# Expert hidden layers in two PSUM banks, combination weights and overflow branch placed earlier, tail rewritten

## The chip, the cores and the metric

The kernel runs on one core of a Trainium2 chip. The metric is the device time of one execution in microseconds (us), median of three runs. The profiled execution is one further run, and every duration below comes from it.

## The reference

The reference is one hybrid decoder layer in float32 for 256 tokens of 1024 columns: a conditioned RMS norm, one combined projection that feeds retention and latent attention, a gated merge, and then a hierarchical mixture of experts, whose result goes through a last RMS norm. The change touches only the experts and the last norm:

```python
h = h + gate2 * hier_moe(u)      # u: (256 tokens, 1024)
# hier_moe: top-1 of 4 groups, top-2 of its 8 experts; for each expert e of 32
#   hid = silu(u @ w1[e]) * (u @ w3[e])      # 1024 -> 256
#   y   = hid @ w2[e]                        # 256 -> 1024
#   out[token] += weight(token, e) * y[token]
out = h * rsqrt(mean(h * h) + 1e-6) * final_norm
```

All 32 experts have to be read: each has three float32 matrices of 1 MB.

## The kernel before

The experts are worked on in eight batches (`bt` 0 to 7) of four experts with 32 token slots each. The four experts of a batch lie side by side on the 128 partitions, as column tiles of 32 slots. For one batch the kernel does this:

- `hidden` calls `hidden_mm` (L1391, matmul L1403) for w1 and then for w3. Both write one PSUM bank, w1 into columns 0 to 255 and w3 into 256 to 511. Then come tanh on ACT (L1495), two products on DVE (L1496, L1497), two transposes on PE (L1501) and a copy on ACT (L1504).
- `combine_weights` (L1450) multiplies the selection matrices with the weights (DVE L1456), transposes them (PE L1457) and copies the result to `GT` (ACT L1458).
- `gather` builds the slots of the next batch (DVE L1337 and L1339, PE L1343 and L1354).
- `expert_out` (L1508) multiplies with w2 (PE L1514), applies the gate (DVE L1517) and adds through `GT` into the four banks `fin` (PE L1523), which hold the layer's result: `fin[2*b+h]` is half h of token block b.

After batch 7's `hidden` stands an overflow branch (L1546 to L1602): each engine reads a count (`values_load`, L1548) and branches (L1549). It is taken only if an expert has over 32 tokens, which is not so in the run profiled.

The tail (from L1605) is w2 of batch 7 in five column pieces q0 to q4, cut at 0, 256, 512, 768, 896 and 1024. `last_mm(q)` multiplies (PE L1622) and applies the gate (DVE L1625). `last_sum(q)` adds through `GT` into `fin` (PE L1632) and squares on ACT (L1635), with a second ACT instruction that reads the accumulated sum; the squares of q3 and q4 are taken together. `last_gain(q)` multiplies a piece in `fin` by the norm's gain into the output tile (DVE L1639). Then the sums go through a reduction and a scale (DVE L1655, L1656), one small DVE step per token block (L1659), a power of -1/2 on POOL per block (L1660), and the scaling of the output: ACT L1664 and DVE L1666 for the first half of the columns, DVE L1668 straight from `fin` for the second. Four transfers of 256 KB go out from SP (L1667, L1669).

What sets the order: weights are loaded by SP in the order of a plan made in a first pass, into 27 SBUF slots; a load is issued when its slot has been released and the load eight issues earlier has landed. Loads of w1, w2 and w3 are issued at L249, the last pieces of w2 at L311. Matmuls of a constant (L387, `keep_warm`) stand between the last batch's quarters of w3. Within the experts, PE and DVE follow a planner that puts an instruction as early as its inputs and engine allow; in the tail DVE, ACT and POOL follow the order in which the code is written. Waits between engines are set by tile: two engines that touch the same PSUM bank wait for each other, whatever the columns.

Of the kernel before, what the change touches and what calls it, by code (L numbers as in the profile page):

```python
# [18 lines left out]
D = 1024  # L19
# [185 lines left out]
def body(ctx, tc, A, out, plan=None):  # L205
# [1183 lines left out]
    ph_of = [None]  # L1389

    def hidden_mm(bt, m, ks):  # L1391

        name = ("w1", "w3")[m]
        ph = ph_of[0]
        cut = (name, bt) in QB
        for k in ks:
            c = k // 2 if cut else 0
            for j in range(4):
# [4 lines left out]
                i = T.matmul(ph.t[32 * j:32 * j + 32, m * 256:(m + 1) * 256], ug[:, k, 32 * j:32 * j + 32], w,  # L1403
# [29 lines left out]
    ph_of[0] = bank()  # L1433
# [29 lines left out]
    def hidden(bt):  # L1463
        if bt:
            ph_of[0] = bank()
        ph = ph_of[0]
# [58 lines left out]

    for bt in range(8):
        hdT = hidden(bt)
# [6 lines left out]
        if bt:  # L1534
            combine_weights(bt)
# [10 lines left out]
    f_s = {n: SL.alloc("f_" + n) for n in ("x2", "u2", "ov", "w1", "w3", "w2", "hid")}  # L1546
    Gov, Gsh = (f_s["hid"].t[:, i:i + 64].rearrange("p (b e) -> p b e", b=2) for i in (1536, 1600))
    many = nc.values_load(cnti[0:1, 0:1], min_val=0, max_val=256)  # L1548
    with tc.If(many > CAP):  # L1549
        V.scalar_tensor_tensor(Gov, rk1, float(CAP), Gt, op0=ALU.is_gt, op1=ALU.mult)  # L1550
        x2 = f_s["x2"].t.rearrange("p (b k q) -> p b k q", b=2, k=8)
        u2 = f_s["u2"].t.rearrange("p (k t) -> p k t", k=8)
        ov = f_s["ov"].t.rearrange("p (b n) -> p b n", b=2)
        V.memset(f_s["ov"].t, 0.0)
        for b in range(2):
            V.tensor_scalar(x2[:, b], hp[:, b], rstd2[:, b:b + 1], None, op0=ALU.mult)
        for k2 in range(4):
            pb = bank()
            for kk in range(2):
                for b in range(2):  # L1560
                    T.transpose(pb.t[:, kk * 256 + b * 128:kk * 256 + (b + 1) * 128], x2[:, b, 2 * k2 + kk, :], ident)
            for kk in range(2):
                k = 2 * k2 + kk
                S.activation(u2[:, k, :], pb.t[:, kk * 256:(kk + 1) * 256], AF.Identity, bias=s2c[:, k:k + 1],
                             scale=a2c[:, k:k + 1])
            pb.free()
        wv = {n: f_s[n].t.rearrange("p (k n) -> p k n", k=8 if n != "w2" else 2) for n in ("w1", "w3", "w2")}
        ft, fh = f_s["hid"].t[:, 0:512], f_s["hid"].t[:, 512:1024].rearrange("p (f t) -> p f t", f=2)
        fy = f_s["hid"].t[:, 1024:1536]
        with tc.For_i(0, 32, 1) as e:  # L1570
            for n in ("w1", "w3", "w2"):
                src = A[n][0].rearrange("g i (p k) n -> (g i) p k n", p=128)
                Q.dma_start(wv[n], src[bass.ds(e, 1)].rearrange("o p k n -> (o p) k n"))
            ph = [bank(), bank()]
            for m, n in enumerate(("w1", "w3")):
                for f in range(2):
                    for k in range(8):
# [5 lines left out]
            for pb in ph:  # L1583
                pb.free()
# [16 lines left out]
    for s in f_s.values():  # L1601
        s.free()  # L1602
# [109 lines left out]
```

## Time and profile before

| | us |
|---|---|
| median of 3 runs | 521.34 (520.93 to 521.62) |
| profiled execution, its own time | 521.56 |
| its span | 519.8 |
| PE busy | 492.7 (95%) |
| DVE busy | 286.4 (55%) |
| ACT busy | 197.9 (38%) |

The profiled execution lies 0.22 us above the median, and 1.8 us of its time lie outside the span. The span is read from its end: the stretch from about 350 us is the expert loop, the stretch from 503 us the tail. For each stretch the table of stretches gives the DMA share (of 16 engines), the GB/s and the clock that TensorE was granted; the waits say what an engine stood still for; the timeline gives the tail instruction by instruction.

### The profile page before, as it was taken

To read this page: it belongs to the slowest core of one execution; us is meant where nothing else is said; L and a number is where in the kernel's file an instruction comes from. 1 tells how busy PE (TensorE), PEld (TensorE's weight loads), DVE (VectorE), ACT (ScalarE), POOL (GpSimd) and SP (SyncE) were. 2 spreads that over 40 slices of the span, in tenths; PEclk is the share of its full clock that TensorE was granted. 3 is DMA by queue.
4 is the path that set the end of the run, shared out by engine and by line. 5 is a ranking of instruction groups with operands and counts; after the bars stand their busy time and mean duration, and the time that the engine had idled before them with its cause. 6 is when DMAs were issued, how large, how long until landed. Compare 5 with 4: busy or idle time off the path is not lost.

```text
span 519.8 us, 8582 instructions
## 1 busy us (share of the span) xinstructions
PE 492.7 (95%) x3440; PEld 339.1 (65%) x3443; DVE 286.4 (55%) x525; ACT 197.9 (38%) x366; POOL 56.8 (11%) x50
## 2 busy tenths in 40 slices
PE   6899999999999999999999999999999989898994
PEld 2678999997887878888688887443344343434432
DVE  3455789884696987979966746414031313131213
ACT  3545773454677544557434424202020211121013
POOL 1000321411000001119800000000000000000000
PEclk9999999999999999999999999999999999999999
DMA  9999899788876782998689888999999999999992
GB/s 272 323 320 361 297 353 398 289 321 312 333 242 244 247 321 81 338 396 308 234 342 352 311 352 301 417 386 422 420 417 419 421 415 419 421 419 416 392 325 99
DMA packets 68097, 174.85 MB, mean 336 GB/s; under 512 B 5422, under 2 KB 27091, under 8 KB 57816
## 3 DMA queue, kind: packets, MB, share of 16 engines
q1 hardware_dynamic: 65602, 174.01, 89.8%
q10 hardware_dynamic: 2454, 0.27, 0.4%
q8 instruction: 28, 0.46, 0.4%
q14 instruction: 13, 0.11, 0.1%
HBM read 173.22 MB, written 1.05 MB: 335 GB/s over the span
## 4 chain that ended last, share of the span: by engine, by line
PE 74%; DVE 8%; DMA 6%; SPq 5%; ACT 3%; issue 2%; POOL 1%; ACTq 1%; DVEq 0%; POOLq 0%
PE b L1403 11%; PE b L378 8%; PE b L380 8%; PE b L379 8%; PE b L1514 6%; PE b L1523 5%; PE b L1343 5%; SPq L249 3%; DVE s L464 3%; DMA s<-in_w_in 2%; SPq L241 2%; DMA s<-in_w 2%; PE b L1354 1%; PE b L1543 1%; ACT s L463 1%
## 5 line engine op out<-in xcount | busy, mean ns | idle before, releaser
L464 DVE TENSOR_TENSOR s<-s,s 128x1024 fp32r<-128x1024 f32 (+2 forms) x92 | 110.9, 1219 | 41.5 <-ACT s L463 40.5
L463 ACT ACTIVATE s<-s 128x1024 fp32r<-128x1024 f32 (+2 forms) x92 | 83.3, 922 | 86.9 <-PE b L380 53.7
L378 PE MATMUL b<-s,s 128*128 128x512 f32 (+2 forms) x258 | 102.2, 396 | 1.3 <-ACT s L463 1.3
L380 PE MATMUL b<-s,s 128*128 128x512 f32 (+2 forms) x258 | 99.4, 385 | 1.3 <-DVE s L464 1.3
L379 PE MATMUL b<-s,s 128*128 128x512 f32 (+2 forms) x258 | 98.1, 380 | 0.0
L1403 PE MATMUL b<-s,s 128*32 128x256 f32 x1024 | 61.4, 380 | 0.0
L378 PEld LDWEIGHTS b<-s,s 128*128 128x128 f32 x258 | 48.5, 188 | 15.6 <-ACT s L463 4.4
L380 PEld LDWEIGHTS b<-s,s 128*128 128x128 f32 x258 | 48.4, 188 | 13.2 <-DVE s L464 3.8
L379 PEld LDWEIGHTS b<-s,s 128*128 128x128 f32 x258 | 48.5, 188 | 8.5 <-issue 0.2
L1403 PEld LDWEIGHTS b<-s,s 128*32 128x32 f32 x1024 | 32.8, 110 | 31.1 <-issue 9.9
L1061 DVE SCALAR_TENSOR_TENSOR s<-s,cs,s 128x1024 f32<-128x1024 f32 x32 | 41.4, 1293 | 0.3
L532 PE MATMUL b<-s,s 128*128 128x256 f32 x128 | 36.2, 284 | 0.5 <-DVE s L464 0.5
L530 PE MATMUL b<-s,s 128*128 128x256 f32 x128 | 36.4, 285 | 0.0
L531 PE MATMUL b<-s,s 128*128 128x256 f32 x128 | 36.1, 283 | 0.0
L1495 ACT ACTIVATE wr<-b 128x256 f32<-128x256 f32 x8 | 3.1, 383 | 78.5 <-PE b L1403 73.7
L1514 PE MATMUL b<-s,wr 128*32 128x512 f32 x224 | 32.8, 596 | 0.0
L1343 PE MATMUL b<-s,sml 128*128 128x512 f32 x56 | 26.9, 603 | 5.3 <-DVE sml L1339 5.3
L1337 DVE TENSOR_TENSOR S<-cst,rk 128x128 f32<-128x128 f32 x16 | 4.1, 287 | 48.9 <-PE b L1457 48.9
L1130 POOL TENSOR_TENSOR s<-s,s 128x1024 f32<-128x1024 f32 x8 | 25.8, 3260 | 13.0 <-DVE s L464 13.0
L1523 PE MATMUL b<-s,rt 128*128 128x512 f32 x56 | 26.2, 611 | 0.0
L372 ACT ACTIVATE s<-b 128x512 f32<-128x512 f32 (+2 forms) x25 | 14.1, 568 | 31.0 <-PE b L1343 12.5
L532 PEld LDWEIGHTS b<-s,s 128*128 128x128 f32 x128 | 24.4, 191 | 0.9 <-DVE s L464 0.9
(258 smaller groups left out, 654.7 us busy)
## 6 DMA issues: line engine op xcount, KB each, us to landing
s<-in_w SPq DMA_DIRECT2D x92, 1024.0 KB
s<-in_w_in SPq DMA_DIRECT2D x22, 1024.0 KB
s<-in_w_ada SPq DMA_DIRECT2D x16, 1024.0 KB
s<-in_w_ada SPq DMA_DIRECT2D x16, 512.0 KB
s<-in_w_mla_o SPq DMA_DIRECT2D x4, 1024.0 KB
s<-in_w_ret_o SPq DMA_DIRECT2D x4, 1024.0 KB
s<-in_w_out SPq DMA_DIRECT2D x4, 1024.0 KB
s<-in_w SPq DMA_DIRECT2D x6, 512.0 KB
```

The lines of the kernel that those rows point to most:

```text
L378: T.matmul(o, l[0], r[0], start=start, stop=False, skip_group_check=True)
L379: T.matmul(o, l[1], r[0], start=False, stop=False, skip_group_check=True)
L380: return T.matmul(o, l[0], r[1], start=False, stop=stop, skip_group_check=True)
L463: S.activation(hi, src, AF.Copy)
L464: V.tensor_tensor(lo, src, hi, ALU.subtract)
L530: T.matmul(o, hi[:, f], mh, start=k == 0 and c == 0, stop=False, skip_group_check=True)
L532: T.matmul(o, lo[:, f], mh, start=False, stop=k == 7, skip_group_check=True)
L1061: V.scalar_tensor_tensor(a, t[:, kk, :], cs[:, k:k + 1], a, op0=ALU.mult, op1=ALU.add)
L1343: T.matmul(pg[k4].t, Sr[:, b], hp[:, b, 4 * k4:4 * k4 + 4, :].rearrange("p k q -> p (k q)"), start=b == 0, stop=b == 1, skip_group_check=True)
L1403: i = T.matmul(ph.t[32 * j:32 * j + 32, m * 256:(m + 1) * 256], ug[:, k, 32 * j:32 * j + 32], w, start=k == 0, stop=k == 7, skip_group_che ...
L1514: T.matmul(py[n].t[32 * j:32 * j + 32, :], hdT[:, k, 32 * j:32 * j + 32], ts[j][:, k, n * 512:(n + 1) * 512], start=k == 0, stop=k == 1, s ...
L1523: T.matmul(fin[2 * b + n].t, GT[:, b * 128:(b + 1) * 128], y[:, n * 512:(n + 1) * 512], start=bt == 0, stop=bt == 7, skip_group_check=True)
```

## The change

It has four parts. First, `hidden` takes two banks, one for w1 and one for w3; tanh and the first product are written between the two sets of matmuls. Second, `combine_weights(bt)` for batches 1 to 7 is called before `hidden(bt)` instead of behind it. Third, the overflow branch becomes a function, with its body as it was, that is called before `hidden(7)`. Fourth, the tail: PE joins the engines whose order is written by hand; `last_sum(2)` comes before `last_mm(3)`; q3 and q4 are squared separately, q4 of block 1 on DVE (a copy and a product with accumulation); `last_gain` is applied to q2 and q3 too, ahead of `last_sum(4)`; one step and one power serve both blocks; ACT scales 512 columns of each block, DVE 384 and then 128 out of `fin`; one of the four output transfers is issued from ACT's queue.

```diff
-    ph_of = [None]
+    ph_of = [None, None]
...
-        ph = ph_of[0]
+        ph = ph_of[m]
...
-                i = T.matmul(ph.t[32 * j:32 * j + 32, m * 256:(m + 1) * 256], ug[:, k, 32 * j:32 * j + 32], w,
+                i = T.matmul(ph.t[32 * j:32 * j + 32, 0:256], ug[:, k, 32 * j:32 * j + 32], w,
...
         if bt:
-            ph_of[0] = bank()
-        ph = ph_of[0]
+            ph_of[:] = bank(), bank()
+        p1, p3 = ph_of
...
+            if m == 0:
+
+                S.activation(ht, p1.t[:, 0:256], AF.Tanh, scale=0.5)
+                V.scalar_tensor_tensor(ht, ht, 1.0, p1.t[:, 0:256], op0=ALU.add, op1=ALU.mult)
+                p1.free()
...
-        S.activation(ht, ph.t[:, 0:256], AF.Tanh, scale=0.5)
-        V.scalar_tensor_tensor(ht, ht, 1.0, ph.t[:, 0:256], op0=ALU.add, op1=ALU.mult)
-        V.tensor_mul(ht, ht, ph.t[:, 256:512])
-        ph.free()
+        V.tensor_mul(ht, ht, p3.t[:, 0:256])
+        p3.free()
...
     for bt in range(8):
+        if bt:
+            combine_weights(bt)
+        if bt == 7:
+            overflow()
         hdT = hidden(bt)
...
-        if bt:
-            combine_weights(bt)
...
     def last_sum(q):
         for b in range(2):
             T.matmul(fp[b][q], GT[:, b * 128:(b + 1) * 128], y[:, piece[q]], start=False, stop=True, skip_group_check=True)
-            if q != 3:
-                f = fp[b][q] if q < 3 else fin[2 * b + 1].t[:, 256:512]
-                S.activation(sq, f, AF.Square, accum_out=ssf[:, b, min(q, 3):min(q, 3) + 1])
+            f, w = fp[b][q], cut[q + 1] - cut[q]
+            if (q, b) == (4, 1):
+                V.tensor_copy(sq2, f)
+                V.scalar_tensor_tensor(sq2, sq2, 1.0, sq2, op0=ALU.mult, op1=ALU.mult, accum_out=ssf[:, b, q:q + 1])
+            else:
+                S.activation(sq[:, 0:w], f, AF.Square, accum_out=ssf[:, b, q:q + 1])
...
-    tail.enter_context(tc.manual_schedule(engines={V.engine, S.engine, G.engine}))
+    tail.enter_context(tc.manual_schedule(engines={T.engine, V.engine, S.engine, G.engine}))
...
+    last_sum(2)
     last_mm(3)
-    last_sum(2)
     last_mm(4, (0,))
     last_sum(3)
     last_mm(4, (1,))
-    V.tensor_reduce(s3, ssf[:, :, 0:3], AX.X, ALU.add)
+    last_gain(2)
+    V.tensor_reduce(s3, ssf[:, :, 0:4], AX.X, ALU.add)
     V.tensor_scalar(s3, s3, 1.0 / D, EPS, op0=ALU.mult, op1=ALU.add)
+    last_gain(3)
     last_sum(4)
-    for b in range(2):
-        V.scalar_tensor_tensor(tf[:, b:b + 1], ssf[:, b, 3:4], 1.0 / D, s3[:, b:b + 1], op0=ALU.mult, op1=ALU.add)
-        G.tensor_tensor(rf[:, b:b + 1], tf[:, b:b + 1], mhalf[:, 0:1], ALU.pow)
+    V.scalar_tensor_tensor(tf, ssf[:, :, 4], 1.0 / D, s3, op0=ALU.mult, op1=ALU.add)
+    G.tensor_tensor(rf, tf, mhalf[:, 0:2], ALU.pow)
     for b in range(2):
         r = rf[:, b:b + 1]
-        m = 512 if b else 256
-        S.activation(o[:, b, 0:m], o[:, b, 0:m], AF.Copy, scale=r)
-        if b == 0:
-            V.tensor_scalar(o[:, b, m:512], o[:, b, m:512], r, None, op0=ALU.mult)
-        Q.dma_start(out[0, b * 128:(b + 1) * 128, 0:512], o[:, b, 0:512])
-        V.scalar_tensor_tensor(o[:, b, 512:1024], fin[2 * b + 1].t, r, fnb[:, 512:1024], op0=ALU.mult, op1=ALU.mult)
+        S.activation(o[:, b, 0:512], o[:, b, 0:512], AF.Copy, scale=r)
+        V.tensor_scalar(o[:, b, 512:896], o[:, b, 512:896], r, None, op0=ALU.mult)
+        V.scalar_tensor_tensor(o[:, b, 896:1024], fp[b][4], r, fnb[:, 896:1024], op0=ALU.mult, op1=ALU.mult)
+        (S if b else Q).dma_start(out[0, b * 128:(b + 1) * 128, 0:512], o[:, b, 0:512])
         Q.dma_start(out[0, b * 128:(b + 1) * 128, 512:1024], o[:, b, 512:1024])
```

Behind the change the lines are: tanh L1483, first product L1484, second product L1500, transposes L1504, branch L1533 and L1534, `last_mm` L1628 and L1631, `last_sum` L1638 (copy L1641, product with accumulation L1642, squares L1644), `last_gain` L1648, reduction and scale L1665 and L1666, step L1669, power L1670, scaling L1673 to L1675, output L1676 and L1677.

The first place is PE between batch 7's hidden layer and its last layer. In the rows, `wr` is the hidden tile, `rt` is `GT`, `S` the selection matrices and `cnti` the count. Before:

```order
L1501 MATMUL b_4159<-cst,wr 128x128 [waits DVE_49,PE_49]
L1501 MATMUL b_4159<-cst,wr 128x128
...
L1457 MATMUL b_4168<-cst,S_2752 128x128 [waits PE_49]
L1457 MATMUL b_4168<-cst,S_2752 128x128
L1548 TENSOR_LOAD cnti [waits DVE_49]
L1549 COMPARE_AND_BRANCH
...
L1622 MATMUL b_4308<-s_3915,wr 32x256 [waits DVE_49,DMAHW6_49,PE_49,Activation_49]
L1622 MATMUL b_4308<-s_3915,wr 32x256 x3
```

Now:

```order
L1533 TENSOR_LOAD cnti [waits DVE_49]
L1534 COMPARE_AND_BRANCH
...
L1504 MATMUL b_4305<-cst,wr 128x128 [waits DVE_49]
L1504 MATMUL b_4305<-cst,wr 128x128
...
L1628 MATMUL b_4316<-s_3921,wr 32x256 [waits DMAHW6_49,Activation_49]
L1628 MATMUL b_4316<-s_3921,wr 32x256 x3
L1628 MATMUL b_4316<-s_3921,wr 32x256 [waits DMAHW7_49]
```

The count and the branch now stand ahead of batch 7's hidden layer, and the transposes L1457 have left this place as well, so that the first piece's matmuls follow the hidden tile's copy and the constant's matmuls.

The second place is DVE in the tail, from q4's multiplication to the first scaling (before, one row earlier). The `b` tiles of L1648 are the banks of `fin`, `sml` are the small sums. Before:

```order
L1625 TENSOR_TENSOR s_3078<-b_4350,s_664 128x128 [waits PE_49]
L1625 TENSOR_TENSOR s_3078<-b_4364,s_664 128x128 [waits PE_49]
L1655 TENSOR_REDUCE sml<-sml 128x2 [waits Activation_49]
L1656 TENSOR_SCALAR sml<-sml 128x2 [waits DVE_49]
L1659 SCALAR_TENSOR_TENSOR sml<-sml 128x1 [waits DVE_49,Activation_49]
L1659 SCALAR_TENSOR_TENSOR sml<-sml 128x1 [waits Activation_49]
L1666 TENSOR_SCALAR s_4167<-s_4167,sml 128x256 [waits Pool_49]
```

Now:

```order
L1631 TENSOR_TENSOR s_3079<-b_4372,s_664 128x128 [waits PE_49]
L1648 TENSOR_TENSOR s_4313<-b_3076,s_3856 128x256 [waits Activation_49]
L1648 TENSOR_TENSOR s_4313<-b_3078,s_3856 128x256 [waits Activation_49]
L1665 TENSOR_REDUCE sml<-sml 128x2
L1666 TENSOR_SCALAR sml<-sml 128x2 [waits DVE_49]
L1648 TENSOR_TENSOR s_4313<-b_3076,s_3856 128x128
L1648 TENSOR_TENSOR s_4313<-b_3078,s_3856 128x128
L1641 COPY s_3856<-b_3078 128x128 [waits DMAHW1_49,PE_49]
L1642 SCALAR_TENSOR_TENSOR s_3856,sml<-s_3856 128x128 [waits DVE_49]
L1669 SCALAR_TENSOR_TENSOR sml<-sml 128x2 [waits DVE_49,Activation_49]
L1674 TENSOR_SCALAR s_4313<-s_4313,sml 128x384 [waits Pool_49]
```

Four gains (two of 256 and two of 128 columns) now stand between the multiplication of q4 (L1631, here the first row) and the squares of q4's block 1 (L1641, L1642), and there is one small step for both blocks instead of two.

The third place is PE in the tail, from the first half of q4's weights to the last sums; `b_3075` and `b_3077` before, and `b_3076` and `b_3078` now, are the second halves of `fin`. Before:

```order
L1622 MATMUL b_4350<-s_3961,wr 32x128 x3
L1622 MATMUL b_4364<-s_3961,wr 32x128 [waits DMAHW6_49,PE_49]
L1632 MATMUL b_3075<-s_3078,rt 128x256 [waits DVE_49]
L1632 MATMUL b_3077<-s_3078,rt 128x256
L1622 MATMUL b_4364<-s_3961,wr 32x128 x3
L1622 MATMUL b_4364<-s_3961,wr 32x128 [waits DMAHW7_49]
L1622 MATMUL b_4364<-s_3961,wr 32x128 x3
L1632 MATMUL b_3075<-s_3078,rt 128x128 [waits DVE_49,Activation_49]
L1632 MATMUL b_3077<-s_3078,rt 128x128 [waits Activation_49]
L1632 MATMUL b_3075<-s_3078,rt 128x128 [waits DVE_49]
L1632 MATMUL b_3077<-s_3078,rt 128x128
```

Now:

```order
L1628 MATMUL b_4362<-s_3974,wr 32x128 [waits DMAHW4_49]
L1628 MATMUL b_4362<-s_3974,wr 32x128 x3
L1628 MATMUL b_4362<-s_3974,wr 32x128 [waits DMAHW5_49]
L1628 MATMUL b_4362<-s_3974,wr 32x128 x3
L1628 MATMUL b_4372<-s_3974,wr 32x128 [waits DMAHW6_49,PE_49]
L1628 MATMUL b_4372<-s_3974,wr 32x128 x3
L1638 MATMUL b_3076<-s_3079,rt 128x128 [waits DVE_49,Activation_49]
L1638 MATMUL b_3078<-s_3079,rt 128x128 [waits Activation_49]
L1628 MATMUL b_4372<-s_3974,wr 32x128 [waits DMAHW7_49]
L1628 MATMUL b_4372<-s_3974,wr 32x128 x3
L1638 MATMUL b_3076<-s_3079,rt 128x128 [waits DVE_49]
L1638 MATMUL b_3078<-s_3079,rt 128x128 [waits DVE_49]
```

The sums of q2 (L1632, 128x256) have left this place, those of q3 stand between the two halves of q4's matmuls, and both of the last sums, q4's, wait for DVE where before only the first did; the instruction that each of them now waits for is the gain of q3 in its own bank.

## Rows read from the trace of the kernel before

**Rows 1.** The page's first line: span and instructions of the profiled execution

```profile
span 519.8 us, 8582 instructions
```

**Rows 2.** Stretches: length, busy us (instructions), granted clock, DMA share, GB/s

```profile
340.00:350.00 10.00, 10.00 (x126) 4.91 (x123) 0.69 (x1) 0.00 (x0) 0.00 (x0) 1.00 0.97 378
...
440.00:480.00 40.00, 36.60 (x343) 16.72 (x346) 9.11 (x26) 6.24 (x14) 0.00 (x0) 1.00 1.01 419
...
500.00:505.00 5.00, 4.00 (x43) 1.96 (x41) 1.22 (x3) 0.77 (x2) 0.00 (x0) 1.00 1.08 322
...
509.50:510.00 0.50, 0.18 (x2) 0.14 (x2) 0.50 (x3) 0.00 (x0) 0.00 (x0) 1.00 0.07 17
510.00:510.25 0.25, 0.25 (x3) 0.12 (x2) 0.25 (x2) 0.00 (x0) 0.00 (x0) 1.00 0.00 0
...
516.00:517.00 1.00, 0.00 (x0) 0.00 (x0) 0.00 (x0) 0.00 (x0) 0.00 (x0) 1.00 1.05 389
517.00:518.00 1.00, 0.00 (x0) 0.00 (x0) 0.00 (x0) 0.00 (x0) 0.00 (x0) 0.81 1.02 379
```

**Rows 3.** SP's queue, 440 to 520 us: waits; us in total, times, longest

```profile
SPq L249 <- DMA s<-in_w: 29.4, 14, 2.1
...
SPq L311 <- PE b L387: 2.5, 2, 1.3
```

**Rows 4.** PE's waits, 350 to 480 us: us in total, times, longest

```profile
PE b L1343 <- DVE sml L1339: 4.5, 6, 1.1
...
PE b L1501 <- DVE wr L1497: 4.3, 3, 1.5
```

**Rows 5.** The chain that ended last: start us, us, what

```profile
501.84 7.84 DMA s<-in_w
```

**Rows 6.** Timeline, tail: start us, us, engine, line, [idle before <- releaser]

```profile
503.18 1.93 PE L1622 MATMUL b<-s,wr 128*32 128x256 f32 x32 [0.85 <-ACTq L1549]
...
506.65 0.73 PEld L1632 LDWEIGHTS b<-s,rt 128*128 128x128 f32 x4 [0.41 <-ACT s L1635]
...
509.18 1.41 DVE L1639 TENSOR_TENSOR s<-b,s 128x256 f32<-128x256 f32 x4
...
509.82 0.38 PE L1622 MATMUL b<-s,wr 128*32 128x128 f32 x2 [0.53 <-DMA s<-in_w]
...
510.13 1.13 PE L1632 MATMUL b<-s,rt 128*128 128x256 f32 x4
...
511.19 0.64 PE L1622 MATMUL b<-s,wr 128*32 128x128 f32 x14
...
511.76 1.19 PE L1632 MATMUL b<-s,rt 128*128 128x128 f32 x8
511.89 0.29 DVE L1625 TENSOR_TENSOR s<-b,s 128x128 f32<-128x128 f32 x1 [1.11 <-PE b L1622]
...
512.28 0.17 DVE L1656 TENSOR_SCALAR sml<-sml 128x2 f32<-128x2 f32 x1
512.82 0.38 ACT L1635 ACTIVATE s<-b 128x256 f32<-128x256 f32 x1 [0.91 <-PE b L1632]
...
513.64 1.04 POOL L1660 TENSOR_TENSOR sml<-sml,mhalf 128x1 f32<-128x1 f32 x2 [197.18 <-DVE sml L1659]
513.83 0.16 DVE L1659 SCALAR_TENSOR_TENSOR sml<-sml 128x1 f32<-128x1 f32 x1 [0.35 <-ACT s L1635]
514.21 1.23 ACT L1664 ACTIVATE s<-s,sml 128x256 f32<-128x256 f32 x2 [0.41 <-POOL sml L1660]
...
514.74 0.36 SPq L1667 DMA_DIRECT2D out<-s  x1
...
516.20 0.41 SPq L1669 DMA_DIRECT2D out<-s  x1
```

**Rows 7.** By form, last 22 us and first 20: busy us, mean ns

```profile
L1664 ACT ACTIVATE s<-s,sml 128x512 f32<-128x512 f32 x1 | 0.7, 721 | 0.0
...
L499 DVE SCALAR_TENSOR_TENSOR s<-s 128x512 f32<-128x512 f32 x2 | 1.3, 684 | 0.0
```

More of the change, by code (lines that the diff above doesn't have):

```diff
@@ L1464, in hidden @@
         if bt:
-            ph_of[0] = bank()
-        ph = ph_of[0]
+            ph_of[:] = bank(), bank()
+        p1, p3 = ph_of
         if bt == 7:
@@ L1544, in body @@
                              start=False, stop=False, skip_group_check=True)
[L1546 to L1554, printed above, removed]
-        for b in range(2):
[L1556 to L1577, printed above, removed]
-                        T.matmul(ph[m].t[:, f * 256:(f + 1) * 256], wv[n][:, k, f::2], u2[:, k, :], start=k == 0,
-                                 stop=k == 7, skip_group_check=True)
-            S.activation(ft, ph[0].t, AF.Tanh, scale=0.5)
-            V.scalar_tensor_tensor(ft, ft, 1.0, ph[0].t, op0=ALU.add, op1=ALU.mult)
-            V.tensor_mul(fh.rearrange("p f t -> p (f t)"), ft, ph[1].t)
-            for pb in ph:
-                pb.free()
-            for b in range(2):
-                for n in range(2):
-                    pb = bank()
-                    for f in range(2):
-                        T.matmul(pb.t, fh[:, f, b * 128:(b + 1) * 128], wv["w2"][:, f, n * 512:(n + 1) * 512],
-                                 start=f == 0, stop=f == 1)
-                    V.tensor_mul(fy, pb.t, g2b[:, n * 512:(n + 1) * 512])
-                    pb.free()
-                    o = ov[:, b, n * 512:(n + 1) * 512]
-                    V.scalar_tensor_tensor(o, fy, Gov[:, b, 0:1], o, op0=ALU.mult, op1=ALU.add)
-            V.tensor_copy(Gsh[:, :, 0:31], Gov[:, :, 1:32])
-            V.tensor_copy(Gov[:, :, 0:31], Gsh[:, :, 0:31])
-        for b in range(2):
-            for n in range(2):
-                T.matmul(fin[2 * b + n].t, ident, ov[:, b, n * 512:(n + 1) * 512], start=False, stop=False,
-                         skip_group_check=True)
@@ L1601, in body @@
-    for s in f_s.values():
-        s.free()
     o = o_s.t.rearrange("p (b n) -> p b n", b=2)
-    ssf = small(8).rearrange("p (b q) -> p b q", b=2)
+    ssf = small(10).rearrange("p (b q) -> p b q", b=2)
     s3, tf, rf = small(2), small(2), small(2)
     fnb = LD.get("fn").t[:, 0:1024]
-    sq = LD.get("fn").t[:, 1024:1280]
+    sq, sq2 = LD.get("fn").t[:, 1024:1280], LD.get("fn").t[:, 1280:1408]
     cut = [0, 256, 512, 768, 896, 1024]
```

59 lines of the change are left out of this document (58 added, 1 removed).

## The prediction

> **What bounds the kernel now.** I read the stretches first, then the waits, then the end. The span is 519.8 us [rows 1]; the profiled execution took 521.56, so 1.8 lie outside it, and the median of the three runs, 521.34, lies 0.22 below it. I sum against the profiled execution and put the difference on the median. From 440 to 480 us all DMA engines are busy (share 1.01) at 419 GB/s, while PE is busy for 36.60 of 40 us [rows 2]: the expert loop runs at the pace of the weights. SP's queue says the same: 29.4 us of its waits from 440 to 520 us were for earlier loads to land, and two late ones for PE's constant matmuls come to 2.5 [rows 3]. So what PE gains in this loop buys only more waiting for weights, unless it makes a load start earlier while the DMA engines stand idle.
>
> At the end the chain runs over a transfer issued by 501.84 that took 7.84 us, so landed at 509.68 [rows 5]; PE had stood for 0.53 us when it took this data at 509.82 [rows 6]. From there 10 us remain to the end of the span. These are the chain on which the tail has to be judged: q4's matmuls, its multiplication on DVE (511.89), the last sums on PE (511.76, for 1.19), squares on ACT (512.82), the small step on DVE (513.83 for the second block), the power on POOL (513.64, two in 1.04), scaling from 514.21, the first output issue at 514.74, the last at 516.20 [rows 6]. The output is bound by bandwidth: 389 GB/s with share 1.05 [rows 2], which is 0.67 us for each of four 256 KB transfers, 2.7 together, while the four issues lie within 1.5 us.
>
> **Part 1: two banks, combination weights and branch.** In 350 to 480 us, over six batches, PE stood 4.5 us for the selection matrices and 4.3 for the hidden product [rows 4]. Two banks let tanh and the first product run beside w3's matmuls, and the weights' two transposes, two DVE products and one ACT copy per batch now stand ahead of the hidden layer, so I expect most of these 8.8 us to go from where they are. They come back as waits for weights, because the DMA share was already 1.01; the work that hides the moved instructions is the same load stream. Value: 0. One place could differ: from 340 to 350 us DMA moved 378 GB/s instead of 419 [rows 2], so about 10 x 41/419 = 1.0 us of transfer time was lost there, around batch 0's w2, whose slots PE releases. PE's work up to that release changes by one wait less and two transposes earlier for the next batch. Its bounds are -1.0 (the whole gap) and +0.3 (the last matmuls on two sides of it as they overlap); I take 0, since the matmuls of batch 0 in front of the release are the same.
>
> The branch cost PE 0.85 us in front of the last layers, at 503.18 [rows 6]. It now costs about as much in front of batch 7's hidden layer, where queued behind it are w1's matmuls, and behind those the quarters of w3, which arrive at DMA's pace, with matmuls of a constant between them. Cost there: 0 to 0.85, I take 0. With the branch, tanh, a product and two transposes gone, q0's matmuls can start up to 2 us before 503.18. That gain ends at the landing at 509.68, since PE already waited there. Value: 0.
>
> **Part 2: the tail.** What leaves the path: the sums of q2, which took PE from 510.13 to 511.19, 1.06 us [rows 6], now come before q3; in their place stand q3's sums, half of the eight instructions of 1.19, so 0.6. q4's first half then runs from 509.82 to about 510.2, q3's sums to 510.8, q4's second half to 511.2 (its data had arrived: no transfer ran after 510.00 [rows 2]), and q4's multiplication starts near 511.3, 0.6 before the 511.89 of now.
>
> What enters: DVE's order is written by hand, and behind this multiplication it has two gains of 256 columns, reduction, scale, and two gains of 128. PE's last sums wait for the gain of q3 in their bank. By durations that is 0.29 (multiplication) + 2 x 0.35 (a quarter of 1.41 for four gains) + 2 x 0.17 + 0.29 = 1.62 us to the end of the first short gain [rows 6]. DVE overlaps the starts of its instructions: multiplication and reduction together took 0.39, from 511.89 to 512.28 [rows 6], not 0.46, so I take 1.45. The gains end at 512.75 and, 0.2 later, 512.95. PE's two sums (0.6, half of the eight) then end at 513.25 and 513.48, against 512.95 for the last one now.
>
> Then block 1 goes over DVE: a copy of 128 columns (0.29 as the multiplication of that width) and a product with accumulation. The nearest row for that is 512 columns in 0.684 [rows 7]; for 128 I take 0.33, between a quarter of it and the whole. So the one small step starts at 513.55 + 0.29 + 0.33, near 514.2, in place of 513.83. From that step's start to the power's end the second block took 0.85 (513.83 to 513.64 + 1.04) [rows 6], so the scalings start at 515.08 in place of 514.21: +0.87. Here one power instead of two gives nothing, because the first of two was what the scaling of now waited for.
>
> The first output transfer waits for ACT's 512 columns, 0.72 [rows 7], in place of 256 columns, 0.51 (1.23 less 0.72): +0.21. DVE's 384 and 128 columns run beside that. Four transfers follow at 0.67 each, as before; issuing one from ACT's queue saves nothing on a stream that is bound by bandwidth. Sum: +0.87 + 0.21 = +1.08, so 521.34 + 1.08 = **522.4**. The bounds of the small terms (0.2 on the gains, -0.16 to +0.35 on the product, 0.2 on PE's overlaps) give 522.0 to 523.0.
>
> **The page rule that speaks against it.** That PE waits for another engine in the same bank is seen now: at 506.65 the second sums stood 0.41 us for a square of other columns [rows 6]. The Trainium skill, page "PSUM — Partial Sum Buffer", section "PSUM bank collisions raise a hardware error", says that engines must be kept apart by bank and 32-partition quadrant, not by address. By that rule the gain of q3 and the sum of q4, which use different columns of one bank, must follow each other, and the trace agrees with its 0.41 us; without it the sum would be the 521.8 of the first rival.
>
> **Rivals.** (a) *The gains do not hold PE.* If the sums start right behind the multiplication, they end at 512.2, but DVE still runs its four gains up to 512.95 before the copy. The copy then starts 0.6 earlier than in my sum: +0.5, 521.8, no measurable change. Against it: the wait of 0.41 in the same bank. For it: the sums above are made of overlapping instructions, and DVE may be quicker by some tenths.
>
> (b) *The weights land earlier: faster.* SP waited twice, 2.5 us in all, for PE's constant matmuls before issuing late pieces [rows 3]. If these waits are what put the last landing at 509.68, an earlier PE moves it by up to 2.5, and the time becomes 521.34 - 2.5 + 1.08 = 519.9. With the gap of 1.0 at batch 0 also closed it is 518.9. It turns the sign from 1.08 us of earlier landing on. Against it: DMA share was 1.08 from 500 to 505, and from 509.50 to 510.00 it was 0.07, one of sixteen engines, still moving 17 GB/s [rows 2]; the last landing is one engine's backlog, which an earlier issue does not shorten.
>
> (c) *TensorE's clock falls.* PE will stand for about 1.5 us before the last sums, and more often before q1 to q4. If the clock goes from 2.4 to 1.2 GHz, the 2.2 us of PE work from 509.82 on (0.4 + 0.6 + 0.4 + 0.7) doubles: 524.6. Against it: the clock was 1.00 still at 516 to 517, four us after the last matmul, and fell in 517 to 518 (0.81) [rows 2]; no gap in the new order is that long. [...]
>
> (d) *The two banks don't overlap.* If tanh and the first product stay behind w3's matmuls, or a bank comes free late, the loop still follows the weights: 522.4 as forecast.
>
> **How the numbers follow.** A measurement of this kernel can tell about 0.2%, 1.04 us, from no change, so the forecast, +1.08, lies on that line. Forecast with (d): 0.62; of its range, 522.0 to 523.0, six tenths lie above 522.38, so 0.38 slower and 0.24 same. (a) 0.20, same. (b) 0.11, of which 0.09 faster and 0.02 same, where the landing moves by less than it could. (c) 0.07, slower. Together: faster 0.09, same 0.46, slower 0.45. The likeliest one's own range is 522.0 to 523.0. To hold 8 in 10 the range takes in (a) and landing times that shift by some tenths, down to 520.8, and the upper half of the small terms, up to 523.4; (c) and most of (b) stay out.
>
> **What would show it.** Right: in the last layers, the last landing stays near 510; q4's multiplication starts near 511.3; the last sums stand over a us for DVE's gains; the step starts near 514.2, the scaling near 515.1, the first output issue near 515.8; PE's waits for weights grow in the loop by what the waits of [rows 4] lose. Wrong: a last landing earlier by a us or more (b), last sums directly behind the multiplication (a), a granted clock under 1.00 before 515 (c), or a DMA share that drops in the loop.

## The result: slower, and by more than forecast

| | median, us | ratio to before, 95% interval |
|---|---|---|
| before (9 runs) | 521.78 | |
| changed (9 runs) | 526.15 (523.36 to 527.55) | 1.0079 (1.0058 to 1.0100) |

The forecast was 522.4 with a range up to 523.4. The profiled execution of the changed kernel took 526.15, with a span of 524.5 against 519.8 [rows 1], so 4.7 us more. The two traces divide these 4.7 us into three: the multiplication of q4 starts at 513.87 instead of 511.89 (+1.98), from there to the first output issue it takes 4.74 instead of 2.85 (+1.89), and from the issue to the end of the span 5.89 instead of 5.06 (+0.83).

The timeline of the changed kernel's tail, which answers to [rows 6] (start us, us, engine, line, operation, [idle before <- releaser]):

```profile
510.56 1.13 PE L1638 MATMUL b<-s,rt 128*128 128x256 f32 x4 [0.55 <-DVE s L1631]
...
512.76 0.68 PE L1638 MATMUL b<-s,rt 128*128 128x128 f32 x4 [0.29 <-DVE s L1631]
...
513.38 0.43 PE L1628 MATMUL b<-s,wr 128*32 128x128 f32 x8
...
513.87 0.29 DVE L1631 TENSOR_TENSOR s<-b,s 128x128 f32<-128x128 f32 x1 [1.25 <-PE b L1628]
...
514.08 0.74 DVE L1648 TENSOR_TENSOR s<-b,s 128x256 f32<-128x256 f32 x2
...
515.00 0.48 DVE L1648 TENSOR_TENSOR s<-b,s 128x128 f32<-128x128 f32 x2
...
515.34 0.71 PE L1638 MATMUL b<-s,rt 128*128 128x128 f32 x4 [1.54 <-DVE s L1648]
...
516.82 0.16 DVE L1669 SCALAR_TENSOR_TENSOR sml<-sml 128x2 f32<-128x2 f32 x1
517.13 0.70 POOL L1670 TENSOR_TENSOR sml<-sml,mhalf 128x2 f32<-128x2 f32 x1 [199.87 <-DVE sml L1669]
517.86 1.33 ACT L1673 ACTIVATE s<-s,sml 128x512 f32<-128x512 f32 x2 [1.57 <-POOL sml L1670]
...
518.61 0.36 SPq L1676 DMA_DIRECT2D out<-s  x1
```

Before their last sums (515.34) PE stands 1.54 us for the gains on DVE. Two waits stand ahead of it: 0.55 for q2's multiplication and 0.29 for q3's. PE's waits from 500 to 520 us (us in total, times, longest) hold these and no wait for weights, where [rows 6] had one of 0.53:

```profile
PE b L1638 <- DVE s L1648: 1.5, 1, 1.5
PE b L1638 <- DVE s L1631: 0.8, 2, 0.5
```

The weights were there. In this stretch (columns as in [rows 2]) the DMA engines move the last of them, at 8 GB/s and none behind it, and PE takes the second half of q4 at 513.38:

```profile
510.50:511.00 0.50, 0.44 (x2) 0.42 (x3) 0.50 (x3) 0.00 (x0) 0.00 (x0) 1.00 0.03 8
```

So at the last layers PE was the late one. Its way there, from the sums of batch 6 (L1526) over the broadcast of the last norm's gain (L1472, one row of the array) and batch 7's w1 and w3 (L1403) to q0's matmuls, first in the changed kernel, then the two rows of the kernel before that answer to the first and the third:

```profile
484.47 3.70 PE L1526 MATMUL b<-s,rt 128*128 128x512 f32 x8
...
488.26 0.38 ACT L1458 ACTIVATE rt<-b 128x256 f32<-128x256 f32 x1 [8.03 <-PEq L1534]
...
489.10 1.98 PE L1472 MATMUL b<-s,one 1*128 1x512 f32 x4 [0.93 <-ACTq L1534]
...
491.01 6.16 PE L1403 MATMUL b<-s,s 128*32 128x256 f32 x80
...
504.68 1.93 PE L1628 MATMUL b<-s,wr 128*32 128x256 f32 x32
```

```profile
483.53 3.70 PE L1523 MATMUL b<-s,rt 128*128 128x512 f32 x8
...
489.44 1.98 PE L1472 MATMUL b<-s,one 1*128 1x512 f32 x4
```

Behind the sums, which end at 488.17, ACT copies `GT`, then takes its branch, and PE waits for that 0.93 us. Then come L1472 and 80 matmuls in 6.16 us. The granted clock (the column ahead of the DMA share) in these stretches was:

```profile
490.00:491.00 1.00, 1.00 (x3) 0.18 (x1) 0.00 (x0) 0.60 (x1) 0.00 (x0) 0.98 1.01 373
...
491.00:492.00 1.00, 1.00 (x13) 0.54 (x16) 0.69 (x1) 0.00 (x0) 0.00 (x0) 0.50 1.05 385
...
493.00:494.00 1.00, 1.00 (x13) 0.40 (x9) 0.00 (x0) 0.00 (x0) 0.00 (x0) 0.50 1.04 381
...
494.00:495.00 1.00, 1.00 (x20) 0.56 (x16) 0.00 (x0) 0.00 (x0) 0.00 (x0) 0.81 1.04 371
```

It fell to 0.50, the lower of TensorE's two levels (1.2 GHz), for over three us just as w1's matmuls ran. In the kernel before L1472 stood in the midst of w1's matmuls and the clock was 1.00, as in this stretch right behind L1472:

```profile
491.00:492.00 1.00, 1.00 (x13) 0.42 (x16) 0.55 (x1) 0.19 (x1) 0.00 (x0) 1.00 1.04 385
```

In the loop, the waits of [rows 4] went from 8.8 us to 5.0; L1343 now waits for the first product, which frees the bank:

```profile
PE b L1343 <- DVE wr L1484: 3.0, 3, 1.0
PE b L1504 <- DVE wr L1500: 1.8, 3, 0.6
```

### The profile page after: what moved, and what is told of

The parts are those of the page before. It is cut to its first block, busy times and chain, and to the rows that moved or that the text cites. A ratio compares the mean times of both kernels' runs of the same rounds, so it can differ in the third digit from the quotient of the medians.

```text
span 524.5 us, 8605 instructions
## 1 busy us (share of the span) xinstructions
PE 500.1 (95%) x3443; PEld 340.5 (65%) x3443; DVE 288.7 (55%) x532; ACT 198.1 (38%) x368; POOL 56.5 (11%) x49
## 3 DMA queue, kind: packets, MB, share of 16 engines
HBM read 173.22 MB, written 1.05 MB: 332 GB/s over the span
## 5 line engine op out<-in xcount | busy, mean ns | idle before, releaser
L1403 PE MATMUL b<-s,s 128*32 128x256 f32 x1024 | 63.1, 388 | 0.0
L378 PEld LDWEIGHTS b<-s,s 128*128 128x128 f32 x258 | 48.5, 188 | 14.4 <-ACT s L463 3.3
L380 PEld LDWEIGHTS b<-s,s 128*128 128x128 f32 x258 | 48.4, 188 | 13.5 <-DVE s L464 4.6
L379 PEld LDWEIGHTS b<-s,s 128*128 128x128 f32 x258 | 48.6, 188 | 8.6 <-issue 0.2
L1403 PEld LDWEIGHTS b<-s,s 128*32 128x32 f32 x1024 | 32.7, 112 | 31.2 <-issue 9.8
L1517 PE MATMUL b<-s,wr 128*32 128x512 f32 x224 | 35.4, 597 | 0.0
L1343 PE MATMUL b<-s,sml 128*128 128x512 f32 x56 | 27.7, 614 | 3.4 <-DVE wr L1484 3.0
L1526 PE MATMUL b<-s,rt 128*128 128x512 f32 x56 | 26.2, 610 | 0.0
L1484 DVE SCALAR_TENSOR_TENSOR wr<-wr,b 128x256 f32<-128x256 f32 x8 | 3.4, 420 | 40.4 <-ACT wr L1483 40.4
L1458 ACT ACTIVATE rt<-b 128x256 f32<-128x256 f32 x8 | 3.1, 384 | 58.9 <-PE b L1457 34.8
L532 PEld LDWEIGHTS b<-s,s 128*128 128x128 f32 x128 | 24.4, 191 | 0.7 <-DVE s L464 0.7
L530 PEld LDWEIGHTS b<-s,s 128*128 128x128 f32 x128 | 24.5, 191 | 0.1
```

What stands on the lines that cost most here:

```text
L378: T.matmul(o, l[0], r[0], start=start, stop=False, skip_group_check=True)
L379: T.matmul(o, l[1], r[0], start=False, stop=False, skip_group_check=True)
L380: return T.matmul(o, l[0], r[1], start=False, stop=stop, skip_group_check=True)
L530: T.matmul(o, hi[:, f], mh, start=k == 0 and c == 0, stop=False, skip_group_check=True)
L532: T.matmul(o, lo[:, f], mh, start=False, stop=k == 7, skip_group_check=True)
L1343: T.matmul(pg[k4].t, Sr[:, b], hp[:, b, 4 * k4:4 * k4 + 4, :].rearrange("p k q -> p (k q)"), start=b == 0, stop=b == 1, skip_group_check=True)
```

## Experiments

The times of a line are medians; the ratios are against runs of the kernel before on the same chip and in the same job, whose medians were 521.21, 521.16, 520.72 and 520.96 in the four jobs.

| kernel | median, us | ratio, 95% interval |
|---|---|---|
| e1: changed, branch back | 524.07 | 1.0055 (1.0035 to 1.0075) |
| e2: changed, tail of before | 521.89 | 1.0011 (0.9995 to 1.0027) |
| e3: before, branch ahead | 521.12 | 0.9996 (0.9986 to 1.0005) |
| e4: changed, four matmuls behind the branch | 525.38 | 1.0095 (1.0063 to 1.0127) |
| e5: before, two banks and combination weights | 520.10 | 0.9981 (0.9971 to 0.9990) |
| e6: before, tail | 524.68 | 1.0071 (1.0054 to 1.0088) |
| e7: e6, outputs from SP alone | 523.70 | 1.0050 (1.0032 to 1.0068) |
| e8: e6, gains behind the power | 522.81 | 1.0033 (1.0021 to 1.0044) |
| e9: before, two banks | 520.64 | 0.9996 (0.9986 to 1.0005) |
| e10: e5, no constant's matmuls between the quarters | 521.08 | 1.0005 (0.9996 to 1.0015) |
| e11: e10, another order of the tail | 520.36 | 0.9996 (0.9986 to 1.0005) |
| e12: e8, planner's order on PE | 523.10 | 1.0037 (1.0023 to 1.0052) |

### The branch and the tail taken apart: e1 to e4

My theory behind the result (T) was that the moved branch makes PE rest, that the clock then falls, and that PE therefore arrives late at the last layers. Its rivals: the loop's new order makes PE late (R), or the tail alone costs (S).

**e1**, the branch back behind the hidden layer:

```diff
-        if bt == 7:
-            overflow()
         hdT = hidden(bt)
...
+    overflow()
     o = o_s.t.rearrange("p (b n) -> p b n", b=2)
```

> The changed kernel with one thing undone: the overflow branch stands behind batch 7's hidden layer again. Theory T (the branch ahead of the hidden layer leaves a gap of 0.9 us on TensorE, the clock falls to half for 3.4 us, and the chain over the last layers becomes later than the last weights): granted clock 1.00 from 485 to 500 us, the last layers start 1.5 us earlier against the last landing than in the changed kernel, time about 524.0, 2 us below the changed kernel. Rival R (the new order of the expert loop makes TensorE late): time within 0.5 us of the changed kernel's 526.1. Rival S (only the tail costs): the same as R, 526.

Measured: 524.07, ratio 1.0055 against 1.0079, so the branch looks worth 0.24%, 1.3 us, though the two intervals overlap. In its trace the clock is 1.00 from 480 to 505, q0's matmuls start at 501.87, and yet the last sums end at 513.52 and wait 1.5 us for the gains as before. T's number for it, 524.0, was right, but 2.9 us of the loss stay.

**e2**, the tail of the kernel before in the changed kernel (the tail's lines replaced by the old ones).

> The changed kernel with the tail of the kernel before; two banks, combination weights and the moved branch stay. Theory T: the clock falls behind the branch as in the changed kernel, the last layers start as late, and only the tail's 1.9 us from the last multiplication to the first output issue come back: 524.2. Rival S (only the tail costs): 521.8, the time before. Rival R as T: 524.2, but with the clock at 1.00.

Measured: 521.89, ratio 1.0011. The tail makes up 3.5 of the 4.1 us. So T's number for it (524.2) was wrong and S's nearly right, though the clock fell just as T had it. PE's timeline in e2:

```profile
488.93 1.98 PE L1472 MATMUL b<-s,one 1*128 1x512 f32 x4 [0.93 <-ACTq L1534]
...
490.83 6.21 PE L1403 MATMUL b<-s,s 128*32 128x256 f32 x80
...
504.55 0.64 PE L1628 MATMUL b<-s,wr 128*32 128x256 f32 x8
```

q0's matmuls start as late as in the changed kernel, and the old tail makes it good by being 2.4 us shorter from there to its last sum (8.95 us from 504.55 to 513.50, against 11.37).

**e3**, only the branch ahead, in the kernel before (the body as a function, called as in the changed kernel).

> The kernel before with one part alone: the overflow branch stands ahead of batch 7's hidden layer. Theory T: the clock falls to half around 490 us for some 3 us, which costs 1.7 us of work, the branch costs the same 0.9 in its new place, and 0.5 us of the old wait for the last weights takes a part back: 1.0 to 1.5 us above before, 522.8 to 523.3. Rivals R and S: no change, 521.8.

Measured: 521.12, ratio 0.9996: no change, as R and S had it. The mechanism of T is there all the same, in the timeline and in one stretch:

```profile
487.46 1.95 PE L1472 MATMUL b<-s,one 1*128 1x512 f32 x4 [0.40 <-PEq L1530]
...
489.34 6.21 PE L1403 MATMUL b<-s,s 128*32 128x256 f32 x80
...
503.67 1.71 PE L1624 MATMUL b<-s,wr 128*32 128x256 f32 x27
```

```profile
490.00:491.00 1.00, 1.00 (x14) 0.46 (x10) 0.14 (x1) 0.00 (x0) 0.00 (x0) 0.50 1.05 387
```

PE rests 0.40 us, L1472 comes next, the clock is 0.50, and the 80 matmuls take 6.21 us. But with the old cost of 0.85 at 503.18 [rows 6] gone, q0 starts at 503.67, only 0.5 later, and the wait of 0.53 for the last weights takes that up. The gap is 0.40 here and 0.93 in e2 and the changed kernel, because there ACT has the copy of `GT` ahead of its branch (at 488.26 in the changed kernel, right behind batch 6's sums, which still read the old `GT`; e5's row below names them as what it waits for). Two parts of the change, harmless apart, meet at this place.

**e4**, work for PE between the branch and L1472:

```diff
             overflow()
+            keep_warm(4)
         hdT = hidden(bt)
```

> The changed kernel with four matmuls of a constant on TensorE between the branch and the two broadcasts of the last norm's gain. Theory T: if the clock's fall can be kept off by work at this place, the clock is 1.00 from 490 to 495 us, 1.7 us of work come back, the four matmuls cost 1.0, time 525.4. If the fall was already settled by the gap: clock as in the changed kernel and time 0.5 to 1 above it, 527. Rivals R and S: clock without effect, 526 to 527.

```profile
488.08 1.03 PE L387 MATMUL b<-oneb 128*128 128x512 bf16 x3 [0.93 <-ACTq L1534]
...
490.95 4.52 PE L1403 MATMUL b<-s,s 128*32 128x256 f32 x80
```

```profile
491.00:492.00 1.00, 1.00 (x21) 0.62 (x24) 0.69 (x1) 0.00 (x0) 0.00 (x0) 1.00 1.05 387
```

The clock stayed at 1.00 (the row of L387 shows three of the four added matmuls), although PE still rested 0.93 us: in this one profile the rest alone did not bring the clock down. The 80 matmuls took 4.52 us instead of 6.16 to 6.21, so the fall costs 1.7 us of PE's time. In the whole time this does not show: the ratio, 1.0095, is not below the changed kernel's 1.0079, though the median in us is the one that T expected. The runs scatter from 524.3 to 527.9. As a saving this run is inconclusive.

### The two halves alone, and the tail's terms: e5 to e8

**e5**, two banks and combination weights with branch and tail as before: e1's and e2's edits together.

> Two banks and earlier combination weights alone; branch and tail as before. The forecast's theory (the weights' landing hides whatever the loop gains): 521.2, no change. Theory L (the new order of the loop and the branch both make TensorE late at the last layers): 521.2 too, but with the scatter of the run that keeps the moved branch gone. Theory G (the loop's gain shows once the branch does not throw the clock down): 520.0 or less.

Measured: 520.10, ratio 0.9981, faster than the kernel before by 1.0 us, and the fastest of all. G (520.0 or less) comes nearest. The timeline (batch 7's w1 with L1472 in its midst, the copy of `GT`, q0's first matmuls):

```profile
487.03 2.35 PE L1403 MATMUL b<-s,s 128*32 128x256 f32 x34
487.20 0.38 ACT L1458 ACTIVATE rt<-b 128x256 f32<-128x256 f32 x1 [8.03 <-PE b L1526]
...
489.31 1.98 PE L1472 MATMUL b<-s,one 1*128 1x512 f32 x4
...
501.98 1.93 PE L1628 MATMUL b<-s,wr 128*32 128x256 f32 x32 [0.40 <-ACTq L1534]
```

From the end of batch 6's sums (487.10) to q0 it takes 14.9 us, 16.6 in e2 and 15.9 before (487.23 to 503.18). Here too PE never waits for weights in the last layers. It could not have gained without them: in this profile they were earlier as well. The last thin rest of the stream, 17 GB/s at 509.50:510.00 in [rows 2], comes two us sooner, and from 340 to 350 us, the place that the prediction named, the DMA engines moved 411 GB/s instead of 378:

```profile
340.00:350.00 10.00, 10.00 (x125) 5.30 (x126) 2.40 (x8) 0.77 (x2) 0.00 (x0) 1.00 1.01 411
...
507.50:508.00 0.50, 0.50 (x19) 0.39 (x11) 0.36 (x2) 0.00 (x0) 0.00 (x0) 1.00 0.08 18
```

In that stretch at 340 us the eight profiles with two banks have 383 to 419 GB/s, the six with one bank 364 to 398. How much of the earlier landing is owed to the two banks and how much to the run, one profile each does not tell. So the part that I had valued at 0 is worth 1 us, and the moved branch takes it back: e2 against e5 is 0.30%, 1.6 us.

**e6**, the tail alone in the kernel before (the changed kernel's tail lines).

> The tail alone, in the kernel before. Theory V (TensorE's order by hand and DVE's gains make the chain from the first piece's matmuls to the last sum 11.4 us long instead of 9.8, and behind it the output takes 1.35 more): the last sum ends at 514.5 instead of 512.9, time 524.2. The forecast's theory (the chain is held by the last landing; +1.1): 522.3.

Measured: 524.68, ratio 1.0071, 3.7 us: V was right, the forecast's +1.1 wrong.

```profile
502.97 1.93 PE L1622 MATMUL b<-s,wr 128*32 128x256 f32 x32 [0.85 <-ACTq L1549]
...
513.64 0.71 PE L1632 MATMUL b<-s,rt 128*128 128x128 f32 x4 [1.54 <-DVE s L1642]
...
515.43 0.70 POOL L1664 TENSOR_TENSOR sml<-sml,mhalf 128x2 f32<-128x2 f32 x1 [199.18 <-DVE sml L1663]
...
516.91 0.36 SPq L1670 DMA_DIRECT2D out<-s  x1
```

From q0 (502.97) to the end of the last sums (514.35) it takes 11.4 us, against 9.8 in [rows 6] (503.18 to 512.95): +1.6. From there to the first issue 2.56 against 1.79: +0.8. This is the profile of a run that took 523.75; the other three took 524.65 to 524.77.

**e7**, the same with all outputs from SP:

```diff
-        (S if b else Q).dma_start(out[0, b * 128:(b + 1) * 128, 0:512], o[:, b, 0:512])
+        Q.dma_start(out[0, b * 128:(b + 1) * 128, 0:512], o[:, b, 0:512])
```

> As the tail alone, with one thing changed: all four output transfers are issued from SP. Theory Q (the transfer from ACT's queue makes one DMA engine land 0.6 to 0.8 us after the other fifteen on the last transfer): the sixteen landings of the last transfer lie within 0.1 us, time 0.6 to 0.7 below the tail alone, 523.5. Rival (chance or the length of the stream): the straggler stays, 524.2.

Measured: 523.70 (523.29 to 523.85), 1.0 below e6, though the intervals of the ratios overlap. The last transfer of the changed kernel ends late. The first rows are the changed kernel's last stretches, the one behind them is of the kernel before:

```profile
522.00:522.50 0.50, 0.00 (x0) 0.00 (x0) 0.00 (x0) 0.00 (x0) 0.00 (x0) 0.50 0.54 201
522.50:523.00 0.50, 0.00 (x0) 0.00 (x0) 0.00 (x0) 0.00 (x0) 0.00 (x0) 0.50 0.01 4
```

```profile
518.00:518.50 0.50, 0.00 (x0) 0.00 (x0) 0.00 (x0) 0.00 (x0) 0.00 (x0) 0.50 0.74 275
```

At the full rate of 381 GB/s just ahead, 201 over half a us mean that data stopped moving near 522.3 there, and the span ends at 524.5, 2.2 us later; before, 275 after 369 mean about 518.4, and the span ended at 519.8, 1.4 later. SP's waits for the outputs come to 3.2 us in the changed kernel and to 1.9 in e7, as before.

In the trace, one of the sixteen completions of the last transfer comes 0.79 us after the others in the changed kernel, 0.61 in e1 and 0.65 in e4, all with one output on ACT's queue; in e6, e8 and e12, which have it too, and in all eight kernels with SP alone, the last two completions lie within 0.02 in the profiled run. So ACT's queue brings a late completion in some runs and not in others: Q fits the times (three of e6's four runs lie 0.8 above all of e7's), but the profile of e6 itself had no straggler. It is likely and not proved.

**e8**, the gains of q2 and q3 behind the power:

```diff
     last_mm(4, (1,))
-    last_gain(2)
     V.tensor_reduce(s3, ssf[:, :, 0:4], AX.X, ALU.add)
     V.tensor_scalar(s3, s3, 1.0 / D, EPS, op0=ALU.mult, op1=ALU.add)
-    last_gain(3)
     last_sum(4)
...
     G.tensor_tensor(rf, tf, mhalf[:, 0:2], ALU.pow)
+    last_gain(2)
+    last_gain(3)
```

> As the tail alone, with the gains of q2 and q3 put behind the power on DVE instead of ahead of the last sums. Theory W (the wait of the last sums for the gains in their bank is on the path, 1.3 to 1.5 us): TensorE's last sums start within 0.2 us of the last multiplication's end, DVE makes the gains while POOL computes the power, time 1.2 below the tail alone, 523.0. Rival (the gains only change places on DVE's path): the same time as the tail alone.

Measured: 522.81, ratio 1.0033, 1.9 below e6 in the medians. W was right:

```profile
512.61 0.68 PE L1632 MATMUL b<-s,rt 128*128 128x128 f32 x4 [0.51 <-DVE sml L1658]
...
514.14 1.15 DVE L1642 TENSOR_TENSOR s<-b,s 128x256 f32<-128x256 f32 x4
514.38 0.70 POOL L1662 TENSOR_TENSOR sml<-sml,mhalf 128x2 f32<-128x2 f32 x1 [198.13 <-DVE sml L1661]
...
515.86 0.36 SPq L1670 DMA_DIRECT2D out<-s  x1
```

The last sums now start 0.51 us after PE is ready, not 1.54, and DVE's four gains (1.15) run while POOL computes the power. The first output issue comes at 515.86 instead of 516.91, with q0 at the same 502.98. So the wait that the prediction named is real and worth 1.05 us in the traces; the rest of the 1.9 lies in e6's three other runs.

### What is late: e9 to e12

**e9**, two banks alone: e5 with `combine_weights` at its old place.

> Two banks alone; combination weights, branch and tail as before. If the 1.1 us that the loop's two parts gained together come from tanh and the first product leaving the chain in front of the last layers (0.8 us), this alone gives 520.3. If they come from the transposes of the combination weights leaving it (0.4 us and the copy's join with the branch), it gives 520.8 or more. The forecast's theory (the weights' landing hides it): 521.2.

Measured: 520.64, ratio 0.9996: no change, and the 520.3 was not reached. The intervals of e5 and e9 overlap at their ends (0.9986 to 0.9990), so how the gain splits between the two parts stays open.

**e10**, e5 without the constant's matmuls between the quarters of w3:

```diff
-WARM7 = 3, 3, 3, 3
+WARM7 = 3, 0, 3, 3
```

> The loop's two parts (as in the run with the loop alone) without the constant's matmuls between the last quarters of w3. Theory P (at the last layers TensorE is the late one, not the weights): these matmuls delay it by 0.76 us each time, so the last layers start up to 2 us earlier, until the landing of the last piece holds them: 0.7 to 1.2 below the loop alone, 519.2. Theory of the forecast (the landing holds the end): no change, 520.1. Rival (the gaps throw the clock down): above 520.1, with a granted clock under 1.00 around 490 to 500.

Measured: 521.08, ratio 1.0005: P fell, and "no change" did not come either, since e10 lies 0.24% above e5 and the intervals are apart. q0's matmuls did start 2.5 us earlier than in e5 (499.44 against 501.98), the clock was 1.00 from 480 to 515, and PE's waits from 484 to 515 show where the gain went:

```profile
PE b L1628 <- DMA s<-in_w: 3.3, 5, 1.4
```

3.3 us of waits for weights. SP issued them at the same times as in e5 (the last at 502.29 and 502.27), yet from q2 on they landed 1.5 to 1.6 us later; why is not shown. Here the mechanism of the forecast held: PE early, the landing holds the end. PE and weights arrive within a us or two of each other, and the later of the two decides.

**e11**, e10 with PE's order by hand too, in the order below, and with a square of its own for every piece, all on ACT (those edits are left out here); two powers and the output stay:

```diff
     last_sum(0)
+    last_mm(2, (0,))
     last_sum(1)
-    last_mm(2)
+    last_mm(2, (1,))
     last_gain(0)
-    last_gain(1)
     last_mm(3)
     last_sum(2)
     last_mm(4, (0,))
     last_sum(3)
+    last_gain(1)
     last_mm(4, (1,))
```

> As the run without the constant's matmuls between the quarters, with an order by hand on TensorE in the tail that has no gain behind the last multiplication: q2's sums behind q3's matmuls, q3's sums between the halves of q4, squares of every piece on ACT, two powers, the outputs from SP, as before. If the sums of q2 and q3 really leave the end of the chain: the last sum ends 0.5 to 0.8 earlier, 518.6. If the order by hand costs as much as it saves: the same as that run.

Measured: 520.36, ratio 0.9996, 0.7 below e10 and not below e5. The medians differ by about what was expected, on a base that had lost as much, but the intervals of e10 and e11 overlap: that the order saves anything is not shown.

**e12**, e8 with PE's order in the tail left to the planner (PE taken out of the engines ordered by hand).

> As the run with the gains behind the power, with one thing changed: TensorE's order in the tail is left to the planner, as before, so that a first half of q2's matmuls stands between the sums of q0 and q1 and q2's sums stand between the halves of q4. Theory H (the order by hand adds waits of 0.8 to 1.1 us to the chain where TensorE is the late engine, and the square of q3 in the same bank takes 0.4 of it back): from the first matmul of the last layers to the last sum 9.4 to 9.8 us instead of 10.3, time 522.2. Rival (the landing holds the end): no change, 522.8.

Measured: 523.10, ratio 1.0037, no gain over e8. H fell. From q0 to the end of the last sums it takes 10.56 us, 10.32 in e8. Other waits come in place of those for DVE, one for weights and one for a square in the same bank (and ahead of q1's sums PE's weight load waits 0.41 for a square of q0):

```profile
509.76 0.38 PE L1622 MATMUL b<-s,wr 128*32 128x128 f32 x2 [0.53 <-DMA s<-in_w]
...
512.71 0.89 PE L1632 MATMUL b<-s,rt 128*128 128x128 f32 x4 [0.29 <-ACT s L1638]
```

## Why the prediction was wrong

The direction of the forecast was right and its size was not: 1.08 us forecast, 4.1 measured. In the two traces the time grew by 3.6 us more than forecast; 2.6 of them lie ahead of q4's multiplication (0.6 earlier forecast, 1.98 later measured), 0.2 between it and the first output issue, 0.8 behind that. By its steps:

**"Value: 0" for the loop and "0 to 0.85, I take 0" for the branch** failed. They rested on the one landing wait of 0.53 at the end of the traced run, which I read as proof that PE is always early and the landing fixed at 509.68. Two banks and combination weights alone gain 1.0 us (e5): PE came 1.1 us sooner from batch 6's sums to q0, and in e5's profile the first half of q4 landed at 507.73, so that PE did not stand for it; in e10, with that landing at 509.26, it did, and the gain was gone. Nor is the landing independent of PE: SP's late loads wait for PE to release their slots, and the last load was issued at 503.28 before, at 502.27 in e5 and at 505.00 in the changed kernel. From the view of [rows 3] I took the 2.5 us for the constant's matmuls and left out others for PE, of which this is the longest:

```profile
SPq L249 <- PE b L1354: 4.2, 1, 4.2
```

The branch alone costs nothing (e3), but behind the moved combination weights it leaves a gap of 0.93 us, with the one-row broadcasts next to it the clock falls, 1.7 us of matmul time are lost (e4 against e2), and the time grows by 0.24 to 0.30% (e1, e2 against e5), 1.3 to 1.6 us. That the fall of the clock, and not the gap, makes up this time is not shown, since e4 kept the clock up and saved nothing clear of its scatter. Rival (c) had the right mechanism in the wrong place: I looked for the clock's fall at waits in the tail, where the granted clock stayed 1.00 up to 515. My reason against it, that no gap would be as long as the time from the last matmul to the fall at the end, did not hold: in e3 it fell behind a rest of 0.40 us with the one-row matmuls next to it. The Trainium skill, page "TensorE: Matmul & The Clock Gate", section "HAM oscillation — how this bites in real kernels", warns of gaps between matmuls, in its example waits for DMA that are far longer than these rests. So it does not foretell e3's 0.50, and e4 kept 1.00 behind a longer rest. Rival (b) did not happen in the changed kernel, whose weights were no earlier (they still moved at 510.50), and (d) did not either, since PE's waits in the loop fell from 8.8 to 5.0 us.

**The tail from q4's first half on** was right in most terms: from q4's multiplication to the start of the last sums I had 1.45 us and the trace shows 1.47; from there to the small step 1.4 and 1.48; ACT's 512 columns to the issue 0.72 and 0.75. (514.2 and 0.85 make 515.05 and not 515.08, which changes nothing.) The wait for the gains in the same bank was named: 1.54 us in the changed kernel, 1.05 of which e8 wins back. The rule of the Trainium skill, page "PSUM — Partial Sum Buffer", section "PSUM bank collisions raise a hardware error", that engines are kept apart by bank and not by address, agrees with this 1.54 us, and rival (a), which left it out, fell.

**The start of that chain** failed. I let it begin at the landing, 509.82, and put the multiplication at 511.3, 0.6 earlier than before. Without a landing to hide behind, the chain runs from q0, and the new tail needs 11.4 us for it instead of 9.8 (e6). I had looked at no wait ahead of q4; the waits of 0.55 and 0.29 lie there. Leaving PE to the planner does not win them back (e12), where a wait for weights and waits for the squares of single pieces in the same banks stand instead.

**Two small terms** were missed: the power of two columns takes 0.70 instead of 0.54 us, so "one power instead of two gives nothing" was a loss of 0.16; and "issuing one from ACT's queue saves nothing" was probably a loss of 0.6 to 1.0 in most runs (e7), which is not proved.

The parts add up: +0.71% (tail), -0.19% (loop), +0.24 to 0.30% (branch, with the loop's parts) make 0.76 to 0.82%, against 0.79% measured. (The 0.24 was read off the changed kernel itself; the 0.30 was not. The intervals reach 0.1 to 0.2% to either side.) What is open: why runs with the branch ahead and the loop's parts scatter more (e2 from 519.6 to 523.4) than those with one of them alone, which one profile each cannot tell; and the completion on ACT's queue. The mean granted clock of every run, which is on record, points to the clock but does not settle it: in e2 the four longest runs (522.6 to 523.4) have 0.986 and the other six 0.992 to 0.997, but in the changed kernel a run at 0.984 took 523.55 and three at 0.982 took 526.6 to 527.6. So the fall at w1 may not come in every run; the profiles show it in one run each.

The version to keep is e5: two banks and early combination weights, with the old branch and the old tail, 0.9981 of the kernel before.

## What to carry to other kernels

A wait of half a us at the end of one trace does not make an engine early: ask by how much the other arrival moves from run to run, and price every edit ahead of it as if it were on the path as well. Before an instruction by hand goes between a producer and the last accumulation, look which PSUM bank it touches; work that nobody waits for belongs behind the step that somebody waits for (here behind the power, where it was hidden). And an edit that is free alone should be costed next to the others that move to the same place.

## What the runs showed of the hardware

- In one profile each, TensorE's granted clock went to 0.50 behind a rest of 0.40 us (e3) as well as 0.93 us (e2, changed kernel), each followed by four one-row matmuls of 1.95 to 1.98 us; it stayed at 1.00 behind a rest of 0.93 us when matmuls of the full array came first (e4), and when the one-row matmuls stood in the midst of others (before, e5).
- POOL's power took 0.70 us for 128x2 elements and 0.54 for 128x1.
- An output transfer from ACT's queue beside three from SP came with one completion that was 0.6 to 0.8 us late in three of six profiled runs; with SP alone in none of eight.
- The last pieces of the weights landed 1.5 to 1.6 us later in e10 than in e5, though they were issued within 0.05 us of the same times. Over the fourteen profiles the last one landed between 508.5 and 511.3 us.
